# Head norms of a hybrid decoder trunk: one strip product of unsplit squares for two products of split squares, two strip results in one PSUM bank

## The chip, the cores and the metric

One core of one Trainium2 chip runs the whole kernel. The metric is the device time of one execution in microseconds (us); the number given for a kernel is the median of several executions. A profiled execution also gives the span from its first to its last instruction and the busy time of each engine: PE (TensorE, matmuls), PEld (its weight loads, which overlap with PE), DVE (VectorE), ACT (ScalarE), POOL (GpSimd) and SP (SyncE, which here only issues DMAs).

## What is computed

The trunk has one layer over 2048 tokens of width 1024. An input projection feeds four gated DeltaNet heads and four HGRN2 heads of width 128; each head's output is normed over its 128 channels and gated, the eight heads go through an output projection, and a squared-ReLU MLP and a gated embedding follow. The part that the change touches is the norm of a head's output:

```python
def gated_head_norm(o, w, z):
    o = o * lax.rsqrt(jnp.mean(o * o, axis=-1, keepdims=True) + EPS)
    return o * w.astype(jnp.float32) * jax.nn.silu(z)
...
o_a = gated_head_norm(o_a, gdn_norm[i], z_gdn)      # 4 DeltaNet heads
o_b = gated_head_norm(o_b, hgrn_norm[i], g_hg)      # 4 HGRN2 heads
mix = jnp.concatenate([o_a, o_b], axis=-1)
mix_out = jnp.einsum('btc,cd->btd', mix, w_out[i])
```

Everything is float32, and channels lie on partitions, so the mean over channels is a sum over the 128 partitions, which PE makes with a matrix of ones.

## The kernel before, in words

**Stages.** The 2048 tokens are four blocks q of 512. A first stage (to about 45 us) embeds and norms. The mixer stage (to about 1080 us) makes, for each block, 33 projections of 24 matmuls each (L1176; operands are split into a high and a low part, three matmuls for each of eight 128-row slices) and threads the heads' own work between them. Output projection (L1059, L1210 `mmo`), MLP (L1210 `u`, `d`) and gate (`mmg`) follow.

**Ticks.** PE's order is the order of the code. Each projection is cut into three ticks of eight matmuls (L1176). At the end of a tick the agenda runs one step of each generator that is due. A DeltaNet generator (`gdn_mixer`) and an HGRN2 generator (`hgrn_mixer`) start for each of the four head numbers of a block, 24 ticks after the ones before. `A_STEPS` lists the tick offsets of the DeltaNet steps, `B_STEPS` those of the HGRN2 steps; `A_LAST` and `B_LAST` are those of the last heads (q 3, head 3), where the projections have ended and output projections run instead. The first generators of the next block are a further three ticks off, because a block starts with the projection `ab`. SP's DMAs are issued in code order too. ACT, DVE and POOL are ordered by the scheduler of the language.

**A head's norm.** The last steps of both generators are `finish` and the steps that it takes from `norm_steps`. In the first, ACT squares the 512 columns of the head's output `pso` into `osq` (L613), DVE gates them into `og` (L614), for DeltaNet DVE adds a term (L616), and `split` makes the float32r pair `hl` of a rounded copy (ACT, L176) and a remainder (DVE, L177). In the second, two matmuls of 512 columns with a 128x128 matrix of ones sum both parts over the partitions (L283, L284), ACT copies one row of the result into row 0 of `osq` (L286), and SP stores it to `sd` in DRAM (L288). Then follow, a step each: load of `sd` as 128x4 (L291), scale and power -0.5 (L293 and L172), store to `rd` (L297), load of `rd` on all partitions (L257), multiplication (L622), store to `mixd` (L624). There are 32 such norms, 16 named `h` (HGRN2) and 16 named `g` (DeltaNet).

**Strips.** `strip` (L633) is a matmul with a stationary matrix of 32 columns that writes 32 of PSUM's 128 partitions, at a column position of the array given by `tile_position`. The mixers use strips for products of 32 or 64 columns; several run side by side in the four column positions. A float32 matmul shows as two instructions in the profile, a float32r one as one.

**Level 5 of the DeltaNet solve.** A step writes `psp` by strips, ACT copies it to `part` (L787). The next step writes `pst` and `psx` by strips, each in a quarter of a bank of its own; DVE copies `psx` into `xn` (L799), ACT copies `pst` into `xt` (L801). Level 6 reads `xn` (`psp6`), and one step later `xt` and ACT's `part` (L806) in `psd6`. Banks of the pool `pp` (three of them) go round in the order in which they are asked for.

Of the kernel before, what the change touches and what calls it, by code (L numbers as in the profile page):

```python
# [10 lines left out]
F32 = mybir.dt.float32  # L11
# [3 lines left out]
AF = mybir.ActivationFunctionType  # L15
# [5 lines left out]
P = 128  # L21
# [3 lines left out]
QT = 512  # L25
NQ = T // QT
NC = QT // P
# [4 lines left out]
SB = 32  # L32
# [22 lines left out]

A_STEPS = ((3, 6, 7, 8, 9, 10, 12, 14) + tuple(range(16, 24)) + (24, 26, 28, 30, 32, 34, 36)
           + tuple(o for c in range(38, 54, 4) for o in (c, c + 1.5, c + 2.5))
           + (53, 55, 57, 59, 60, 61, 65, 66))
I_STEPS = (22,)
B_STEPS = (24, 26, 28, 30, 32, 34, 36, 38, 40, 42, 44, 45, 46, 48, 50, 52, 53, 54, 58, 59)  # L60


A_AHEAD = (-12, -6)
# [2 lines left out]
A_FIRST = (3, 7, 8, 8, 9, 10, 12, 14) + tuple(range(16, 24)) + (24, 26, 29, 32, 34, 36, 37)  # L66

A_LAST = (A_STEPS[:16] + (24, 25, 27, 28, 29, 30, 31) + tuple(range(32, 44))
          + (44, 47, 49, 50, 51, 52, 54, 55))
B_LAST = tuple(range(24, 34)) + (35, 36, 37, 39, 41, 42, 43, 44, 46, 47)  # L70
LAST = 44


# [23 lines left out]
def trunk(ctx, tc, x, xT, pT, vecs, w_in, w_ab, gdn_a_log, gdn_dt_bias, w_out, w_up, w_down,  # L97
          w_ple, w_gate, consts, out):
    nc = tc.nc
    V, S, G, PE = nc.vector, nc.scalar, nc.gpsimd, nc.tensor  # L100
# [173 lines left out]
    yod = {q: [dr.tile([P, QT], F32, name=f"yod{q}_{d}") for d in range(KD)] for q in (0, 2, 3)}  # L274
    ple_r = [None] * NQ

    def norm_steps(acc, scale, eps, name, done, pool=None):

        hl = st.tile([P, 2, QT], F32R, tag="hl", name=f"hl_{name}", bufs=1)
        split(hl, V, acc)  # L280
        yield
        ps = bank(f"nrm_{name}", pool or pp)
        PE.matmul(ps, ones, hl[:, 0, :], start=True, stop=False)  # L283
        PE.matmul(ps, ones, hl[:, 1, :], start=False, stop=True)  # L284
        row = acc[0:1, :]
        S.activation(row, ps[0:1, :], AF.Copy)  # L286
        sd = dr.tile([1, QT], F32, name=f"sd_{name}")
        nc.sync.dma_start(sd, row)  # L288
        yield
        m = sm.tile([P, NC], F32, tag="m", name=f"m_{name}")  # L290
# [101 lines left out]
    with ExitStack() as ectx:  # L392
        es = ectx.enter_context(tc.tile_pool(name="es", bufs=1))
        with tc.manual_schedule(engines={mybir.EngineType.SP, mybir.EngineType.Activation, mybir.EngineType.DVE}):
# [44 lines left out]
            done = []  # L439
# [23 lines left out]
    with mixers as mctx:  # L463
# [145 lines left out]
        def finish(q, h, pso, zt, extra, eps, n):  # L609

            og = st.tile([P, QT], F32, tag="late", name=f"og_{n}")
            sq = st.tile([P, QT], F32, tag="acc", name=f"osq_{n}", bufs=3)
            S.activation(sq, pso, AF.Square, scale=P ** -0.5)  # L613
            V.tensor_tensor(og, pso, zt, ALU.mult)  # L614
            if extra is not None:
                V.tensor_tensor(sq, sq, extra, ALU.add)  # L616
            rd = []
            yield from norm_steps(sq, 1.0, eps, n, rd.append)
            yield
            rsb = spread_load(rd[0], n)  # L620
# [14 lines left out]
        def gdn_mixer(q, h, live):  # L635
# [139 lines left out]

            def half_bank(name):
                return bank(f"{name}_{n}", pp)[:, : QT // 4].rearrange("p (a i) -> p a i", a=2)

            psp = half_bank("psp5")
            for p in range(2):
                for g in range(NB):
                    strip(g, psp[rows_of(g), p, rows_of(1 - g % 2)], um[5][:, p, rows_of(g)],
# [1204 lines left out]
```

## Time and profile before

| what | value |
|---|---|
| median of 3 runs | 2638.28 us (2636.36 to 2641.67) |
| the profiled execution's own time | 2641.29 us |
| its span, first to last instruction | 2639.5 us |
| PE busy | 2602.8 us (99%) |
| DVE busy | 1965.0 us (74%) |
| ACT busy | 1463.3 us (55%) |
| granted TensorE clock, mean | 0.999 |

Busy time of PE is made from modelled ends of pipelined matmuls, so 99% means that PE is seldom without an instruction, not that it runs at its peak. What a piece of PE's work costs is read from the distance between the starts of neighbouring instructions; what it waits for from the idle time that the timeline shows in brackets with its releaser.

### The profile page before, as it was taken

The numbers are of one execution on the slowest core, as the hardware profiler recorded it, in microseconds if no ns is written. First come the engines' busy times: TensorE is split into PE (matmuls) and PEld (weight loads), VectorE is DVE, ScalarE is ACT, GpSimd is POOL, SyncE is SP. The second block draws the span as 40 slices with busy tenths as digits, with TensorE's granted clock in tenths as the row PEclk, the third lists the DMA queues.
The fourth block names the chain that finished last, engine by engine and source line by source line (L and its number), as shares of the span: only waits on it lengthen the run. The fifth ranks groups of instructions, "written<-read, shape, count | busy, mean of one in ns | idle before, by whom it ended". The sixth has DMA issues, their size and how long they took to land.

```text
span 2639.5 us, 43913 instructions
## 1 busy us (share of the span) xinstructions
PE 2602.8 (99%) x15593; PEld 2146.0 (81%) x15593; DVE 1965.0 (74%) x4032; ACT 1463.3 (55%) x2991; POOL 137.0 (5%) x147
## 2 busy tenths in 40 slices
PE   8999999999999999999999999999999999999999
PEld 6778788878878888787888888888888888888887
DVE  7778777776777777579988768767877765477775
ACT  7766655465555555566666465555454465565431
POOL 0000000000000000110000000001000001101000
PEclk9999999999999999999999999999999999999999
DMA  8877777767767675764675576665644375677663
GB/s 277 282 258 265 263 256 245 238 222 251 241 213 240 222 237 162 232 203 141 214 236 182 179 233 223 214 211 186 220 150 168 140 245 187 202 252 251 207 223 126
DMA packets 267788, 573.87 MB, mean 217 GB/s; under 512 B 55578, under 2 KB 60152, under 8 KB 250416
## 3 DMA queue, kind: packets, MB, share of 16 engines
q1 hardware_dynamic: 265264, 566.86, 64.5%
q0 software_dynamic: 2304, 4.20, 0.9%
q8 instruction: 123, 2.02, 0.3%
q14 instruction: 97, 0.79, 0.1%
HBM read 410.57 MB, written 160.37 MB: 216 GB/s over the span
## 4 chain that ended last, share of the span: by engine, by line
PE 61%; DMA 2%; issue 2%; DVE 2%; ACT 0%; POOL 0%; SPq 0%; DVEq 0%; POOLq 0%; ACTq 0%
PE d L1210 23%; PE u L1210 23%; PE mmg L1210 7%; PE mm L1176 4%; PE mmo L1059 1%; PE mme L203 1%; DMA yod<-yo 1%; DMA mixT<-mixd 0%; DMA rsb_g<-rd_g 0%; DMA yo<-in_xT_dram 0%; DVE t L177 0%; DMA rd_g<-m_g 0%; DVE acc_o L246 0%; POOL yo L1296 0%; DMA raw_out<-in_w_out_dram 0%
## 5 line engine op out<-in xcount | busy, mean ns | idle before, releaser
L1176 PE MATMUL mm<-xt,w 128*128 128x512 f32 x3072 | 785.5, 401 | 1.6 <-DVE acc_vg L571 0.7
L1176 PEld LDWEIGHTS mm<-xt,w 128*128 128x128 f32 x3072 | 552.8, 188 | 108.3 <-issue 2.1
L1210 PE MATMUL d<-db,da 128*128 128x512 f32 x2688 | 612.8, 389 | 0.0
L1210 PE MATMUL u<-t,wu 128*128 128x512 f32 x2604 | 591.2, 389 | 0.0
L1210 PEld LDWEIGHTS d<-db,da 128*128 128x128 f32 x2688 | 504.5, 188 | 104.8
L1210 PEld LDWEIGHTS u<-t,wu 128*128 128x128 f32 x2604 | 488.7, 188 | 101.5
L230 DVE TENSOR_TENSOR db<-db 128x512 fp32r<-128x512 f32 x224 | 159.5, 712 | 60.0 <-ACT db L229 59.0
L1612 DVE TENSOR_TENSOR u<-u,u 128x512 f32<-128x512 f32 x224 | 150.2, 681 | 52.0 <-PE u L1210 50.4
L229 ACT ACTIVATE db<-db 128x512 fp32r<-128x512 f32 x224 | 140.9, 629 | 67.4 <-DMA db<-hid 63.6
L1210 PE MATMUL mmg<-h2T,wg 128*128 128x512 f32 (+1 forms) x792 | 174.7, 383 | 0.0
L1210 PEld LDWEIGHTS mmg<-h2T,wg 128*128 128x128 f32 x792 | 145.5, 188 | 29.1
L1655 ACT ACTIVATE u<-u 128x512 f32<-128x512 f32 x128 | 80.7, 631 | 152.8 <-DVE u L1612 152.1
L177 DVE TENSOR_TENSOR da<-da 128x512 fp32r<-128x512 f32 x128 | 95.2, 743 | 91.3 <-ACT da L176 89.5
L176 ACT ACTIVATE da<-da 128x512 fp32r<-128x512 f32 x128 | 80.6, 630 | 127.8 <-DMA da<-sumd 100.9
L1210 PE MATMUL mmo<-mixT,w_out 128*128 128x512 f32 x600 | 140.0, 393 | 3.3 <-ACT w_out L176 2.0
L1210 PEld LDWEIGHTS mmo<-mixT,w_out 128*128 128x128 f32 x600 | 113.4, 190 | 28.8 <-DVE w_out L177 2.6
L176 ACT ACTIVATE wu<-a 128x512 fp32r<-128x512 f32 x124 | 75.0, 623 | 55.8 <-DMA a<-in_w_up_dram 52.9
L177 DVE TENSOR_TENSOR wu<-a,wu 128x512 fp32r<-128x512 f32 x124 | 85.9, 694 | 8.3 <-ACT wu L176 8.2
L177 DVE TENSOR_TENSOR da<-dr,da 128x512 fp32r<-128x512 f32 x96 | 68.2, 711 | 23.7 <-ACT da L176 22.2
L1656 ACT ACTIVATE u<-u 128x512 f32<-128x512 f32 x128 | 80.4, 628 | 3.0
L176 ACT ACTIVATE da<-dr 128x512 fp32r<-128x512 f32 x96 | 60.5, 630 | 31.9 <-DMA dr<-in_w_down_dram 21.7
L246 POOL TENSOR_TENSOR acc_y<-acc_y,sq_y 128x512 f32<-128x512 f32 x28 | 37.8, 1351 | 759.5 <-ACT sq_y L245 759.5
(401 smaller groups left out, 3675.4 us busy)
## 6 DMA issues: line engine op xcount, KB each, us to landing
w<-cache_in SPq DMA_DIRECT2D x96, 1024.0 KB
db<-hid SPq DMA_DIRECT2D x224, 256.0 KB
cache_in<-w SPq DMA_DIRECT2D x32, 1024.0 KB
hid<-u SPq DMA_DIRECT2D x128, 256.0 KB
da<-sumd SPq DMA_DIRECT2D x128, 256.0 KB
a<-in_w_up_dram SPq DMA_DIRECT2D x124, 256.0 KB
hid<-ht SPq DMA_DIRECT2D x96, 256.0 KB
dr<-in_w_down_dram SPq DMA_DIRECT2D x96, 256.0 KB
```

The lines of the kernel that those rows point to most:

```text
L176: S.activation(t[:, 0], raw, AF.Copy)
L177: eng.tensor_tensor(t[:, 1], raw, t[:, 0], ALU.subtract)
L203: PE.matmul(ps, a, b, start=i == 0, stop=i == n - 1)
L229: S.activation(t[:, 0], plain(t), AF.Copy)
L230: V.tensor_tensor(t[:, 1], plain(t), t[:, 0], ALU.subtract)
L246: eng.tensor_tensor(acc, acc, sq, ALU.add)
L1059: PE.matmul(ps, w[:, term // 2, k, :], xin[q][k][:, term % 2, :], start=i == 0, stop=i == 3 * KD - 1)
L1176: PE.matmul(ps, *terms[i], start=i == 0, stop=i == nt - 1)
L1210: PE.matmul(ps, a, b, start=start, stop=stop)
L1612: V.tensor_tensor(c[new], c[old], ps, ALU.add)
L1655: S.activation(c[k], c[k], AF.Relu)
L1656: S.activation(c[k], c[k], AF.Square)
```

## The change

The change has three parts.

1. The head norms (`strips=True`, called from `finish`) no longer split the squares. Four float32 strips, one for each 128 tokens, sum `osq` with 32 columns of the ones, each at its own column position; the sums of 128 tokens stand on 32 partitions each. ACT copies the 128x128 result, and in a step of its own SP stores four rows of it, one of each 32 partitions, to `sd`. The norm has one step more. All other norms (`norm_whole`) stay as they were.
2. The step lists get one entry more and other offsets, so that the strips come, where they can, just ahead of strips that were there already. From the first step to the store of `mixd` a DeltaNet norm takes 15 ticks instead of 13 and an HGRN2 norm 18 instead of 13.
3. `psx` and `pst` of level 5 are two parts of one bank.

```diff
-           + (53, 55, 57, 59, 60, 61, 65, 66))
+           + (53, 56, 57, 59, 61, 62, 63, 67, 68))
-B_STEPS = (24, 26, 28, 30, 32, 34, 36, 38, 40, 42, 44, 45, 46, 48, 50, 52, 53, 54, 58, 59)
+B_STEPS = (24, 26, 28, 30, 32, 34, 36, 38, 40, 42, 44, 45, 46, 52, 53, 55, 57, 58, 59, 63, 64)
...
-          + (44, 47, 49, 50, 51, 52, 54, 55))
-B_LAST = tuple(range(24, 34)) + (35, 36, 37, 39, 41, 42, 43, 44, 46, 47)
+          + (44, 46, 47, 49, 50, 51, 52, 54, 55))
+B_LAST = tuple(range(24, 34)) + (35, 36, 37, 38, 39, 41, 42, 43, 44, 46, 47)
...
-    def norm_steps(acc, scale, eps, name, done, pool=None):
+    def norm_in_strips(acc, name):
+
+        yield
+        ps = bank(f"nrm_{name}", pp)[:, :P]
+        for c in range(NC):
+            PE.matmul(ps[c * SB : (c + 1) * SB, :], ones.bitcast(F32)[:, :SB], acc[:, blk(c)], start=True, stop=True,
+                      tile_position=(0, c * SB))
+        S.activation(acc[:, :P], ps, AF.Copy)
+        sd = dr.tile([1, QT], F32, name=f"sd_{name}")
+        yield
+        nc.sync.dma_start(sd.rearrange("o (c n) -> (o c) n", n=P), acc[::SB, :P])
+        yield
+        return sd
+
+    def norm_whole(acc, name, pool):
...
+    def norm_steps(acc, scale, eps, name, done, pool=None, strips=False):
+
+        sd = yield from norm_in_strips(acc, name) if strips else norm_whole(acc, name, pool)
...
-            yield from norm_steps(sq, 1.0, eps, n, rd.append)
+            yield from norm_steps(sq, 1.0, eps, n, rd.append, strips=True)
...
-            def half_bank(name):
-                return bank(f"{name}_{n}", pp)[:, : QT // 4].rearrange("p (a i) -> p a i", a=2)
+            def half_banks(name, count):
+                t = bank(f"{name}_{n}", pp)[:, : count * QT // 4]
+                return t.rearrange("p (m a i) -> m p a i", m=count, a=2)
...
-            psx, pst = half_bank("psx5"), half_bank("pst5")
+            both = half_banks("psx5", 2)
+            psx, pst = both[0], both[1]
```

The step lists show how the order moves only in part; the built programs show it. On PE, before, the norm of the HGRN2 head 0 of block 1 stood between whole matmuls (`mm_1_2` is a projection of block 1, `psb_g`, `psc_g` and `of_g` belong to the DeltaNet state):

```order
L825 MATMUL psb_g_0_2_5047<-r_g_0_2_5006,xt_full 128x128
L1176 MATMUL mm_1_2_5042<-xt_1_3291,w_1_2_4883 128x512 x2
L1176 MATMUL mm_1_2_5042<-xt_2_3399,w_1_2_4883 128x512 x2
L283 MATMUL nrm_h_0_5055<-hl_h_0_5012,ones 128x512
L284 MATMUL nrm_h_0_5055<-hl_h_0_5012,ones 128x512
L1176 MATMUL mm_1_2_5042<-xt_2_3399,w_1_2_4883 128x512
L1176 MATMUL mm_1_2_5042<-xt_3_3402,w_1_2_4883 128x512 x3
L830 MATMUL psc_g_0_2_5081<-w_g_0_2_5049,kt_g_0_3835 128x128
```

In the changed program the same norm stands four ticks later on PE, at the head of strips of the next HGRN2 head (`of_h<-att_h` and `at_all<-hb_h`):

```order
L846 MATMUL psb_g_0_3_5115<-r_g_0_3_5079,xt_full 128x128
L1197 MATMUL mm_1_2_5101<-xt_4_3425,w_1_2_4955 128x512 x3
L1197 MATMUL mm_1_2_5101<-xt_5_3428,w_1_2_4955 128x512
L282 MATMUL nrm_h_0_5123<-osq_h_0_4996,ones 32x128 x4
L652 MATMUL of_h<-att_h_1_5041,one 32x4x16 x4
L652 MATMUL at_all<-hb_h_1_5042,qk_h_1_4784 32x2x16 x16
L1197 MATMUL mm_1_2_5101<-xt_5_3428,w_1_2_4955 128x512 x2
L851 MATMUL psc_g_0_3_5166<-w_g_0_3_5117,kt_g_0_3820 128x128
```

The four strips have joined a stretch of strips that was there before. The DeltaNet norm likewise moves from between whole matmuls to just ahead of the strips of `psx_g`. Of the 32 norms 23 join such a stretch. Nine do not: both norms of head 3 of blocks 0, 1 and 2, whose next heads start three ticks later, and three of the last block (`nrm_g` of head 2, `nrm_h` and `nrm_g` of head 3). On PE of the changed program, this is the HGRN2 norm of head 3 of block 1, alone among whole matmuls:

```order
L846 MATMUL psb_g_3_3_7386<-r_g_3_3_7350,xt_full 128x128
L1197 MATMUL mm_2_1_7360<-xt_4_6506,w_2_1_7217 128x512 x3
L1197 MATMUL mm_2_1_7360<-xt_5_6509,w_2_1_7217 128x512
L282 MATMUL nrm_h_3_7394<-osq_h_3_7273,ones 32x128 x4
L1197 MATMUL mm_2_1_7360<-xt_5_6509,w_2_1_7217 128x512 x2
L851 MATMUL psc_g_3_3_7405<-w_g_3_3_7388,kt_g_3_5995 128x128
```

Here the norm opens a stretch of strips of its own. On ACT the scheduler orders anew. Before, at the start of block 1, the DeltaNet head's exponentials (`cd_g`, `tail_g`, `e_g`, `gf_g`) and two loads of function tables stood ahead of `y_qg`, the convolved q that PE's strips `of_g<-y_qg` read:

```order
L669 ACTIVATE jk_g_0_3_3842,ssk_g_0_3827<-t_kg_0_3830 128x128
L649 ACT_TABLE_LOAD
L649 ACTIVATE cd_g_0_3776<-gf_g_0_3686 128x4
L652 ACTIVATE tail_g_0_3777<-tail_g_0_3777 128x8
L657 ACTIVATE e_g_0_3783<-e_g_0_3783,gcol_3707 128x128 x4
L658 ACTIVATE gf_g_0_3686<-gf_g_0_3686 128x512
L671 ACTIVATE kt_g_0_3835<-t_kg_0_3830,tail_g_0_3777 128x128 x4
L580 ACT_TABLE_LOAD
L580 ACTIVATE y_qg_0_3762<-acc_qg_0_3755 128x512
```

In the changed program `y_qg` comes ahead of the first of these table loads on ACT:

```order
L688 ACTIVATE jk_g_0_3_3827,ssk_g_0_3812<-t_kg_0_3815 128x128
L599 ACTIVATE y_qg_0_3745<-acc_qg_0_3738 128x512
L668 ACT_TABLE_LOAD
L668 ACTIVATE cd_g_0_3760<-gf_g_0_3667 128x4
L671 ACTIVATE tail_g_0_3761<-tail_g_0_3761 128x8
```

At the starts of blocks 2 and 3 `y_qg` stays behind them. In all 16 heads, since `psx` and `pst` share a tile, ACT's first copy into `xt_g` now waits for DVE's copies out of that bank into `xn_g`, which the code asks for first; before, it waited for PE alone.

More of the change, by code (lines that the diff above doesn't have):

```diff
@@ L289, in norm_steps @@
         yield
+        return sd
+    def norm_steps(acc, scale, eps, name, done, pool=None, strips=False):
+        sd = yield from norm_in_strips(acc, name) if strips else norm_whole(acc, name, pool)
         m = sm.tile([P, NC], F32, tag="m", name=f"m_{name}")
@@ L774, in pair_bank @@
                 return bank(f"{name}_{n}", pp)[:, : QT // 2].rearrange("p (a i) -> p a i", a=2)
-            def half_bank(name):
-                return bank(f"{name}_{n}", pp)[:, : QT // 4].rearrange("p (a i) -> p a i", a=2)
-            psp = half_bank("psp5")
+            def half_banks(name, count):
+                t = bank(f"{name}_{n}", pp)[:, : count * QT // 4]
+                return t.rearrange("p (m a i) -> m p a i", m=count, a=2)
+            psp = half_banks("psp5", 1)[0]
             for p in range(2):
```

## The prediction

> **What bounds the kernel now.** I read the table of busy time by stretch first. Its columns are the stretch, its length, then busy us of PE, PEld, DVE, ACT and POOL with their instructions, and last the granted clock, DMA share and GB/s.
>
> ```profile
> 60.00:1080.00 1020.00, 1005.47 (x8573) 829.53 (x8572) 763.89 (x2167) 593.73 (x1545) 58.20 (x66) 1.00 0.72 239
> 1080.00:1260.00 180.00, 174.58 (x754) 141.78 (x754) 142.55 (x220) 115.64 (x188) 15.63 (x17) 0.99 0.63 188
> 1260.00:2639.00 1379.00, 1375.12 (x6090) 1139.47 (x6088) 1011.87 (x1565) 712.40 (x1187) 57.95 (x44) 1.00 0.61 203
> ```
>
> In the mixer stage, the first row, PE is without work for only 1020 - 1005.5 = 14.5 us at full clock, while DVE (75%) and ACT (58%) have room. PE's order is fixed, so a microsecond of PE's work taken out of this stage comes off the end, as later stages are as full. Work taken from DVE and ACT counts only where PE waits for them. PE's waits in this stage come next: who waited, for whom, us in total, times, longest.
>
> ```profile
> PE of_g L633 <- ACT y_qg L580: 2.5, 3, 1.0
> PE psa_g L820 <- DVE S_g L832: 1.9, 4, 0.6
> PE at_all L915 <- DVE acc_vg L572: 1.8, 2, 1.3
> PE at_all L633 <- DVE att_h L933: 1.4, 4, 0.6
> PE psx_g L633 <- ACT osq_g L286: 1.4, 1, 1.4
> ```
>
> No single wait stands out; the norm's own name is in the last row.
>
> **The norm on PE, before.** The timeline of PE in a quiet head (start, duration, line, operation, count):
>
> ```profile
> 403.96 0.39 PE L283 MATMUL nrm_h<-hl_h,ones 128*128 128x512 f32 x1
> 404.19 0.39 PE L284 MATMUL nrm_h<-hl_h,ones 128*128 128x512 f32 x1
> 404.42 1.08 PE L1176 MATMUL mm<-xt,w 128*128 128x512 f32 x4
> 405.33 0.39 PE L830 MATMUL psc_g<-w_g,kt_g 128*128 128x128 f32 x2
> 405.55 0.39 PE L833 MATMUL of_g<-y_qg,S_g 128*128 128x128 f32 x2
> ```
>
> Durations overlap; the cost is from start to start. The norm's pair takes 404.42 - 403.96 = 0.46 us, a projection matmul (405.33 - 404.42)/4 = 0.23, and a float32 matmul of 128 columns (two instructions) 405.55 - 405.33 = 0.22.
>
> **Strips.** No strip of before moves 128 columns in all four column positions, but these groups come close. Each of the last three has eight strips, whose columns are 128, 96, 64 and 32 at the four positions and then 32, 64, 96 and 128, so 160 columns at each position:
>
> ```profile
> 427.55 0.43 PE L633 MATMUL psp_g<-xn_g,um 128*32 128x64 f32 x16
> 427.80 0.31 PE L633 MATMUL at_all<-qk_h,keys_h 128*32 128x32 f32 x16
> 427.93 0.47 PE L633 MATMUL of_g<-y_kg 128*32 128x128 f32 x16
> 428.21 0.47 PE L633 MATMUL of_g<-y_qg,y_kg 128*32 128x128 f32 x16
> 428.49 0.47 PE L633 MATMUL of_h<-y_kg 128*32 128x128 f32 x16
> ```
>
> Such a group takes 0.28 us. At the full matmul's rate, 0.22 us for 128 columns, 160 columns take 0.275: the four positions run fully side by side. The four strips of a norm, 128 columns at each position, are then 0.28 x 128/160 = **0.22 us**. The first row is eight strips of 64 columns, two at each position, again 128 columns: 427.80 - 427.55 = 0.25, so short strips lose a little. One after another the four would be 4 x 0.22 = 0.88, the other bound; I take 0.22, since the long strips of the groups are the nearer ones.
>
> The Trainium skill, page "TensorE: Matmul & The Clock Gate", section "Part 3: Packing small matmuls — row/col tiling", gives three column tiles a measured speedup of 2.38 and not 3. By it four strips would take about 0.22 x 3/2.38 = 0.28 us (an estimate from that page), and the change would save 32 x 0.06 = 1.9 us less. The groups above show no such loss.
>
> **Where strips begin and end.** Going from whole matmuls to strips and back has a price, seen in this stretch:
>
> ```profile
> 411.84 1.16 PE L1176 MATMUL mm<-xt,w 128*128 128x512 f32 x4
> 412.93 0.32 PE L633 MATMUL of_h<-att_h,one 128*32 128x64 f32 x8
> 413.06 0.48 PE L633 MATMUL at_all<-hb_h,qk_h 128*32 128x32 f32 x32
> 413.47 1.19 PE L1176 MATMUL mm<-xt,w 128*128 128x512 f32 x4
> ```
>
> From 411.84 to 413.47 are 1.63 us. Four projection matmuls take 0.91; the strips have 64 + 4 x 32 = 192 columns at each position, 0.34 us. What is left, 0.38 us, is the two changes. It is in the program already for the 23 norms that join a stretch; the nine alone pay it anew.
>
> **First term, PE's own work.** 23 norms: 0.46 - 0.22 = 0.24 us less each, 5.5 us. Nine norms: 0.22 + 0.38 - 0.46 = 0.14 us more each, 1.3 us. Sum **-4.2 us**. Moving the norm within the tick order adds nothing else to PE.
>
> **Second term, waits that go.** In the first head PE stood for 1.4 us, since the bank for `psx` still held the previous norm's result, which ACT copied late:
>
> ```profile
> 175.05 0.27 PE L633 MATMUL pst_g<-xt_g,part 128*32 128x32 f32 x8
> 176.69 0.22 PE L633 MATMUL psx_g<-part,xt_g 128*32 128x32 f32 x2 [1.37 <-ACT osq_g L286]
> 294.57 0.50 PE L283 MATMUL nrm_g<-hl_g,ones 128*128 128x512 f32 x1
> 295.37 0.49 PE L284 MATMUL nrm_g<-hl_g,ones 128*128 128x512 f32 x1 [0.29 <-DVE hl_g L177]
> 295.79 0.25 PE L548 MATMUL ps_gb<-cst,gb 36*128 36x36 f32 x1
> 309.82 0.49 PE L633 MATMUL of_g<-y_kg 128*32 128x128 f32 x16
> 311.31 0.49 PE L633 MATMUL of_g<-y_qg,y_kg 128*32 128x128 f32 x16 [1.00 <-ACT y_qg L580]
> ```
>
> With `psx` and `pst` in one bank and the norm right ahead, `psx` takes the bank of `psp`, which ACT has long read: -1.4. The next rows show the second matmul of a pair late, as DVE's half of the split came late: 295.79 - 294.57 = 1.22 us instead of 0.46. There is no split any more: -0.8. The last two rows are the start of block 1: 311.31 - 309.82 = 1.49 instead of 0.28. In the changed order of ACT `y_qg` comes ahead of a table load, four exponentials and more: -1.2. At the starts of blocks 2 and 3 it stays behind them, and I leave the other 1.5 us of this wait in. Sum **-3.4 us**.
>
> **Third term, work off ACT and DVE.** A norm loses these:
>
> ```profile
> L176 ACT ACTIVATE hl_g<-osq_g x16: 614/632/634, 170.3 to 1069.0; 128x512 fp32r<-128x512 f32 x16
> L177 DVE TENSOR_TENSOR hl_g<-osq_g,hl_g x16: 670/684/693, 171.2 to 1070.5; 128x512 fp32r<-128x512 f32 x16
> L286 ACT ACTIVATE osq_g<-nrm_g x16: 572/587/589, 176.1 to 1072.3; 1x512 f32<-1x512 f32 x16
> L827 ACT ACTIVATE w_g<-psb_g,cc_g 128x128 f32<-128x128 f32 x64 | 23.3, 364 | 79.8 <-PE psb_g L825 79.7
> ```
>
> The new copy is 128x128 from PSUM as in the last row, at most 0.36 us. ACT sheds 32 x (0.63 + 0.59 - 0.36) = 27 us, DVE 32 x 0.68 = 22 us, none of it on PE's path by itself. What it can shorten is the waits for DVE above, 1.9 + 1.8 + 1.4 = 5.1 us. Bounds 5.1 and 0; I take **0**, as the scheduler also orders DVE anew and these waits lie in heads crowded by other loads.
>
> **Fourth term, the new wait of ACT for DVE** (shared bank). The rows around level 5 of a quiet head:
>
> ```profile
> 424.02 0.90 ACT L801 ACTIVATE xt_g<-pst_g 32x64 f32<-32x64 f32 x4
> 425.98 0.45 DVE L799 COPY xn_g<-psx_g 32x64 f32<-32x64 f32 x2
> 428.05 0.57 ACT L806 ACTIVATE part<-psp_g 64x128 f32<-64x128 f32 x2 [0.94 <-PE psp_g L633]
> 433.03 0.43 PE L633 MATMUL psd_g<-xt_g,part 128*32 128x64 f32 x16
> ```
>
> ACT's copies would begin at 426.43, where DVE's end, instead of 424.02. Queued behind them on ACT are `xt_full`, later `keys` and `part`; PE waits for `part` at 433.03, 4.4 us after it is ready today. A shift of up to 2.4 us fits in. Where it doesn't fit, the nearest row is a wait of PE for `part`:
>
> ```profile
> 127.60 0.71 PE L633 MATMUL psd_g<-xt_g,part 128*32 128x64 f32 x16 [0.38 <-ACT part L806]
> ```
>
> Bounds: nothing, and 0.4 us in all 16 heads, 6.4 us. Nearest to nothing, by the 4.4 us; I take two heads, **+0.8 us**.
>
> **At no cost.** SP's store of `sd` no longer waits for ACT in the same step:
>
> ```profile
> SPq L288 <- ACT osq_h L286: 50.1, 15, 8.3
> ```
>
> SP issues weight reloads behind that wait, so they come earlier; PE hardly waits for weights, so I count nothing. The five DMAs of a norm stay five, at unchanged distances but for that one step; the longer lags hold `og` and `osq` longer, 18 of the 24 ticks between heads with two and three buffers, so no head waits for one. `mixd` of the last heads keeps its ticks, so the output projection loads it no later.
>
> **Sum.** -4.2 - 3.4 + 0 + 0.8 = -6.8 us. Against the profiled execution's 2641.29 us (span 2639.5 and 1.8 around it) that is 2634.5. That execution was 3.0 us above the median shown, within the runs' 2636.36 to 2641.67, so I forecast 2638.28 - 6.8 = **2631.5 us**. A measurement of this kernel can tell about 0.2%, 5.3 us, from no change: below 2633.0 is faster, above 2643.6 slower.
>
> **Rivals.**
> - *PE's term alone.* The scheduler's new orders of ACT and DVE bring as many waits as go: -4.2 us, 2634.1, within 0.2%. For it speaks that the waits are scattered over many causes; against it that three of them lose their cause. Chance 0.22.
> - *Lighter engines count.* The 5.1 us go as well: 2626.4. Against it: bursts, not averages, make these waits. Chance 0.10.
> - *Strips overlap less than the groups show:* each norm's strips take 0.25 us, as the eight of `psp_g` did, so the change saves 32 x 0.03 = 1.0 us less: 2632.5. Against it the 0.28 us groups, whose strips are as long as the norm's. Chance 0.05. The skill's page, above, speaks for this rival and would put it at 2633.4.
> - *ACT held by DVE: slower.* Place: `xt_g` behind `xn_g`, and on ACT behind it the copies that PE needs. It decides once DVE's copies come over 4 us later than ACT's do today, the slack at 433.03. With DVE 75% busy and other work ahead of those copies (a DMA-fed subtraction stands there at block starts), each head could lose 0.9 us: 16 x 0.9 = 14.4, less 7.6 gained, 6.8 us slower, 2645.1. Against it the 1.1 us by which DVE's copies (to 426.43) beat `psp_g` (427.55) in the rows above. Chance 0.08.
> - *The change doesn't do what it says:* the strips run one after another. 32 x (0.88 - 0.46) = 13.4, plus 9 x 0.38 = 3.4: 16.8 slower, 2655. The groups speak plainly against it. Chance 0.03.
>
> **How the numbers follow.** The forecast has 0.52. Its own spread, with terms three and four between their bounds, lies across the 2633.0 line, some seven parts in ten below. Faster: 0.37 of it, 0.10 of the lighter engines, 0.06 of the two rivals near the line, 0.53. Slower: 0.09 from the last two, cut a little for 2645.1 being near 2643.6. Same: 0.38. The range from 2626.0 (terms one to three) to 2638.5 (the first rival with most of the fourth term's upper bound) leaves out the last two rivals and part of the others, two in ten.
>
> **What would show it.** Right: starts 0.22 us apart from the norm's strips to the next strips; nine lone norms of about 0.6 us; no waits on `osq_g` or `hl_g` and two, not three, on `y_qg`. Wrong: strips 0.9 us long; PE waiting for `part`, `keys` or `xn_g` in many heads; or idle PE time in the stage above 14.5 us.

## The result, and the profile after

| | median | range | runs |
|---|---|---|---|
| before, beside it | 2638.57 us | 2634.13 to 2644.31 | 20 |
| changed | 2641.78 us | 2637.28 to 2648.33 | 20 |

The ratio is 1.0013 (95% interval 1.0007 to 1.0019): within the 0.2% that the prediction counts as no change, about 3 us slower (an interval of 1.8 to 5.0), and not 7 us faster as forecast. The changed kernel's profiled execution took 2639.28 us (span 2637.4), in the lower third of its runs, and alone would have shown a gain of 2 us on the profiled execution of before. A second profile comes from the repeat e12 below: 2645.81 us, the median of that run. I read both.

The stages of the changed kernel, columns as before:

```profile
60.00:1080.00 1020.00, 1006.91 (x8789) 829.20 (x8788) 749.84 (x2141) 568.14 (x1518) 59.25 (x67) 1.00 0.72 240
1080.00:1260.00 180.00, 172.81 (x743) 140.98 (x742) 140.71 (x217) 117.74 (x190) 14.27 (x16) 0.98 0.63 189
1260.00:2637.00 1377.00, 1373.02 (x6080) 1137.48 (x6078) 1009.48 (x1562) 708.19 (x1182) 58.30 (x44) 1.00 0.61 202
```

DVE lost 14 us in the mixer stage, where 22 were forecast, and ACT 26 of 27. PE still stands 13.1 us there, hardly less than the 14.5 of before, and in the second profile 16.5. The next stage is granted less clock, and the last row stands as it stood. PE's waits in the first of these stretches, first profile:

```profile
PE psa_g L841 <- DVE xs_g L767: 2.7, 1, 2.7
PE of_g L652 <- ACT y_qg L599: 1.5, 2, 1.1
...
PE psp_g L652 <- DMA xn_g<-xd_g: 1.2, 1, 1.2
...
PE mm L1197 <- DMA w<-cache_in: 1.0, 1, 1.0
```

The waits that were to go have gone: none on `osq_g` or `hl_g`, two on `y_qg`. Others stand in their place, and two of them end with a DMA, which none of before did.

**PE's own work** came out as forecast. A norm that joined a stretch of strips, and a lone one:

```profile
716.29 1.16 PE L1197 MATMUL mm<-xt,w 128*128 128x512 f32 x4
717.38 0.43 PE L282 MATMUL nrm_h<-osq_h,ones 128*32 128x128 f32 x8
717.62 0.29 PE L652 MATMUL of_h<-att_h,one 128*32 128x64 f32 x8
717.73 0.48 PE L652 MATMUL at_all<-hb_h,qk_h 128*32 128x32 f32 x32
718.14 1.19 PE L1197 MATMUL mm<-xt,w 128*128 128x512 f32 x4
...
593.44 1.16 PE L1197 MATMUL mm<-xt,w 128*128 128x512 f32 x4
594.53 0.43 PE L282 MATMUL nrm_h<-osq_h,ones 128*32 128x128 f32 x8
594.89 1.19 PE L1197 MATMUL mm<-xt,w 128*128 128x512 f32 x4
```

The stretch took 1.63 us without the norm and takes 718.14 - 716.29 = 1.85 with it: 0.22 us, as predicted. The lone norm takes 594.89 - 593.44 - 0.91 = 0.54 us against 0.60. So 23 x -0.24 + 9 x 0.08 = -4.8 us of PE's work.

**Where the profile says that the gain went.** The table follows the same projection matmul through the executions: its start in the trace, less its start in the profile of before (positive is later).

| start in before, us | 222 | 290 | 402 | 1004 | 1108 | 1255 | 2634 |
|---|---|---|---|---|---|---|---|
| changed, first profile | -2.6 | +2.2 | +1.3 | -4.5 | -4.6 | -2.3 | -2.1 |
| changed, second profile | -1.9 | +4.3 | +3.7 | +0.7 | +2.4 | +4.5 | +4.5 |

Both lose 5 to 6 us between 222 and 290 us, at the end of block 0, and 2 between 1108 and 1255. Over the blocks between, the first gained 5.8 us and the second only 3.0. The later loss lies at one place. At the first MLP matmul `u`, 1213.9 us in before, the differences are still -5.0 and +1.8; two hundred `u` matmuls on they are -2.3 and +4.5. These 2.7 us in both profiles are nearly as much as the 3 us of the result. The granted clock at the end of block 0 and in the output projection, first profile and then, for block 0 alone, second:

```profile
260.00:280.00 20.00, 18.51 (x96) 16.13 (x97) 19.64 (x52) 8.31 (x16) 0.00 (x0) 0.91 0.80 262
1120.00:1140.00 20.00, 16.65 (x66) 13.02 (x65) 13.88 (x23) 16.46 (x25) 2.08 (x3) 0.91 0.56 197
```

```profile
250.00:270.00 20.00, 17.18 (x80) 14.61 (x80) 15.75 (x51) 8.06 (x18) 0.00 (x0) 0.83 0.72 219
```

Of 20 us, 1.8 are lost to the clock at 0.91 and 3.4 at 0.83. Before has such a stretch in the output projection too, at 1117 us, so only what comes on top of it counts as new. How the first of these stalls came about in the first profile, on SP, DVE and PE:

```profile
240.85 1.23 SPq L531 DMA_DIRECT2D raw<-in_w_in_dram  x1
242.13 0.42 SPq L192 DMA_DIRECT2D cache_in<-w  x1
242.65 3.65 SPq L728 DMA_DIRECT2D ud_g<-u_g  x4
246.41 0.41 SPq L316 DMA_DIRECT2D rd_g<-m_g  x1
250.71 0.59 SPq L737 DMA_DIRECT2D sys_g<-ud_g  x1
```

```profile
257.36 0.28 DVE L749 TENSOR_TENSOR pr_g<-cst,sys_g 128x64 f32<-128x64 f32 x1 [4.48 <-DMA sys_g<-ud_g]
```

```profile
261.49 0.46 PE L841 MATMUL psa_g<-S_g,y_kg 128*128 128x128 f32 x2 [2.72 <-DVE xs_g L767]
```

The small stores `ud_g` leave right behind a load of 0.5 MB and a store of 1 MB. SP issues `sys_g` only once they have landed, DVE stands 4.5 us for it, the solve that follows is late, and PE stands 2.7 us. The same stores and the same load in before:

```profile
247.17 2.30 SPq L709 DMA_DIRECT2D ud_g<-u_g  x4
...
250.67 0.53 SPq L718 DMA_DIRECT2D sys_g<-ud_g  x1
```

There the stores left 4.5 us later, and SP could issue `sys_g` 1.2 us behind the last of them; here it took 4.4 us. So `sys_g` left at the same time in both, and the 2.6 us by which PE was ahead at 222 us had brought nothing forward. What held here is how fast SP's transfers landed, which is the first theory below in its first form. The prediction counted nothing for it, and no experiment changed this chain by itself. The experiments ask where else the gain went.

### The profile page after: what moved, and what is told of

It reads as the page before. It is cut to its first block, busy times and chain, and to the rows that moved or that the text cites. A ratio compares the mean times of both kernels' runs of the same rounds, so it can differ in the third digit from the quotient of the medians.

```text
span 2637.4 us, 44254 instructions
## 1 busy us (share of the span) xinstructions
PE 2600.8 (99%) x15785; PEld 2142.8 (81%) x15785; DVE 1946.3 (74%) x4000; ACT 1435.2 (54%) x2959; POOL 137.0 (5%) x147
## 4 chain that ended last, share of the span: by engine, by line
PE 71%; DMA 3%; DVE 3%; issue 2%; ACT 2%; SPq 0%; POOL 0%; DVEq 0%; ACTq 0%; POOLq 0%
PE d L1231 23%; PE u L1231 23%; PE mm L1197 12%; PE mmg L1231 7%; PE mmo L1080 1%; PE mme L203 1%; DMA yod<-yo 1%; DMA sys_g<-ud_g 0%; DMA rd_g<-m_g 0%; DMA b<-h1d 0%; DMA mixT<-mixd 0%; PE psa_g L841 0%; PE of_h L984 0%; PE pss_h L973 0%; PE of_h L983 0%
## 5 line engine op out<-in xcount | busy, mean ns | idle before, releaser
L176 ACT ACTIVATE da<-dr 128x512 fp32r<-128x512 f32 x96 | 60.5, 630 | 28.0 <-DMA dr<-in_w_down_dram 16.8
```

The source lines that it names most:

```text
L176: S.activation(t[:, 0], raw, AF.Copy)
```

## The experiments

The base of before differed from chip to chip (2638.6 to 2644.6 us), so each ratio is against before on the same chip. "Delta heads" in the expectations are the DeltaNet heads (`g`), "the other heads" the HGRN2 heads (`h`). The theories: the gain is lost to SP's queue (first as DMA's pace, later theory Q); to the shared bank; to the longer lags; to VectorE's late work (theory D); or strips save nothing.

The last two columns are sums of idle time in the profiled execution between 60 and 1080 us: PE's waits of every kind, and DVE's waits that ended with a DMA. The last column alone doesn't tell the time: e2, e12 and e16 have as much of it as e3 and stand within 4 us of before, while e4 has less and loses 16. The times follow PE's waits more closely.

| run | median less before, us | ratio (95%) | PE waits | DVE waits for DMA |
|---|---|---|---|---|
| before's own profile | | | 14.4 | 45.4 |
| e1 before, shared bank | +0.4 | 1.0003 (0.9992 to 1.0015) | 14.6 | 51.8 |
| e2 changed, two banks | +0.7 | 1.0007 (0.9997 to 1.0017) | 16.3 | 76.1 |
| e3 before, all lags long | +13.7 | 1.0051 (1.0037 to 1.0065) | 24.0 | 76.2 |
| e4 changed, lags short | +16.0 | 1.0057 (1.0041 to 1.0074) | 25.9 | 66.2 |
| e5 before, delta lags long | -5.7 | 0.9977 (0.9967 to 0.9988) | 10.1 | 50.5 |
| e6 changed, delta strips at 54 | +12.4 | 1.0051 (1.0036 to 1.0065) | 25.9 | 74.0 |
| e7 changed, HGRN2 tail tight | +20.2 | 1.0071 (1.0058 to 1.0084) | 27.8 | 99.9 |
| e8 delta strips at 54, HGRN2 as before | +5.7 | 1.0019 (1.0008 to 1.0030) | 21.1 | 58.5 |
| e9 before, HGRN2 lags long | +12.9 | 1.0050 (1.0034 to 1.0067) | 26.0 | 84.8 |
| e10 delta as changed, HGRN2 as before | -0.9 | 0.9997 (0.9989 to 1.0006) | 14.1 | 49.5 |
| e11 delta as changed, HGRN2 strips at 48 | +4.1 | 1.0015 (1.0006 to 1.0023) | 16.7 | 60.4 |
| e12 changed again | +3.3 | 1.0009 (1.0000 to 1.0018) | 15.7 | 80.9 |
| e13 as e9, HGRN2 DMAs by POOL | +78.2 | 1.0291 (1.0276 to 1.0306) | 62.4 | 135.8 |
| e14 changed, HGRN2 DMAs by POOL | +65.7 | 1.0245 (1.0231 to 1.0259) | 63.9 | 128.8 |
| e15 as e10, `sd_g` half a tick earlier | -2.4 | 0.9991 (0.9982 to 1.0000) | 14.6 | 50.1 |
| e16 changed, both `sd` half a tick earlier | +2.4 | 1.0006 (0.9997 to 1.0015) | 18.4 | 78.1 |
| e17 before less two DMAs | -1.8 | 0.9991 (0.9981 to 1.0002) | 13.0 | 47.2 |
| e18 as e9, less two DMAs | -3.0 | 0.9984 (0.9973 to 0.9995) | 18.5 | 43.5 |

### One part of the change at a time

**e1**, the shared bank put into before, and **e2**, taken out of the changed kernel:

```diff
-            psx, pst = half_bank("psx5"), half_bank("pst5")
+            both = half_banks("psx5", 2)
+            psx, pst = both[0], both[1]
```

> The kernel before with one part of the change alone: psx5 and pst5 in one PSUM bank; all norms stay whole. Theory 1 (the change saves about 7 us of PE work and waits over the blocks, and gives it back in block 0, where DMA sets the pace, and in new PE stalls near the end of the output projection, each with a stretch at half clock behind it): the bank plays no part, 0 within 1 us of before. Theory 2 (ACT's xt_g copies now wait for DVE's xn_g copies in the shared bank, and this is what ate the gain): 3 to 7 us slower than before. Theory 3 (the longer lags of the heads' tails ate it): 0 within 1 us.

> The changed kernel with psx5 and pst5 in two banks again; strips and lags stay. Theory 1: within 1 us of the changed kernel, so about 3 us slower than before. Theory 2 (the shared bank ate the gain): 3 to 7 us faster than the changed kernel, so 0 to 4 us faster than before. Theory 3 (the lags): as theory 1.

e1 gives +0.4 us, with an interval from -2 to +4, and e2 stands 2.5 us below the changed kernel's +3.2, each against before on its own chip. No cost of the bank is shown, and the 3 to 7 us that the second theory asked for show in neither run, though the top of e1's interval reaches 4.

**e3**, the longer lags alone, with whole norms:

```diff
-           + (53, 55, 57, 59, 60, 61, 65, 66))
+           + (53, 56, 59, 61, 62, 63, 67, 68))
-B_STEPS = (..., 45, 46, 48, 50, 52, 53, 54, 58, 59)
+B_STEPS = (..., 45, 46, 52, 55, 57, 58, 59, 63, 64)
```

> The kernel before, with whole norms at their pair of matmuls, but with the changed kernel's offsets for the heads' last steps (delta heads 53, 56, 59, 61, 62, 63, 67, 68, the other heads 46, 52, 55, 57, 58, 59, 63, 64). Theory 1: the later steps alone take away the waits of PE on nrm_g and psx (2.2 us of the trace of before) and cost nothing on PE: 0 to 2 us faster than before. Theory 3 (the lags move SP's stores, the loads behind them and the end of each block, and this ate the gain): 3 to 7 us slower than before.

It lost 13.7 us, twice what even the third theory asked for. The lags are not free, and since the changed kernel has the same lags and loses only 3 us, strips and bank together bring back about 10.

**e4**, strips with the lags of before, so that all 32 are lone:

```diff
-           + (53, 56, 57, 59, 61, 62, 63, 67, 68))
+           + (53, 55, 56, 57, 59, 60, 61, 65, 66))
-B_STEPS = (..., 45, 46, 52, 53, 55, 57, 58, 59, 63, 64)
+B_STEPS = (..., 45, 46, 48, 49, 50, 52, 53, 54, 58, 59)
```

> The changed kernel with strips and the shared bank, but with the offsets of before for the heads' last steps (strips at 55 and 48, no other strips in those ticks; stores at 66 and 59). All 32 norms are then lone strips. Theory 1, by its PE term: 32 lone norms at +0.14 us against the pair are +4.5 us where the changed kernel has -4.2, so about 6 to 9 us slower than the changed kernel, less what block 0 swallows of it (a quarter): +8 to +11 us on before. Theory 3 (the lags ate the gain): 0 to 4 us faster than the changed kernel. A rival to the PE term, that joined strips save nothing: the same as the changed kernel within 1 us.

Slower still, by more than PE's work: 32 lone norms at 0.08 are 2.6 us, while PE's waits grew by 11.5. The largest of them:

```profile
PE at_all L936 <- DVE acc_vg L591: 7.5, 2, 4.3
```

In this kernel one tick, not two, lies between the store of the sums and the load behind it; whether that is the reason is not shown. But short lags are no cure as such.

### Which heads, and which steps

**e5**, of e3 only the first line of the diff (the DeltaNet heads late), and **e9**, only the second (the HGRN2 heads late).

> The kernel before, whole norms, with the changed kernel's later offsets for the delta heads alone (53, 56, 59, 61, 62, 63, 67, 68); the other heads keep 46, 48, 50, 52, 53, 54, 58, 59. With both kinds late the same kernel lost 13.7 us. If the loss is shared by the kinds: 4 to 9 us slower than before. If the other heads' steps, which move by 4 to 5 ticks where the delta heads' move by 1 to 2, make it: within 2 us of before. If the delta heads make it: 11 to 14 us slower.

> The kernel before, whole norms, with the changed kernel's later offsets for the other heads alone (46, 52, 55, 57, 58, 59, 63, 64); the delta heads keep 53, 55, 57, 59, 60, 61, 65, 66. Both kinds late gave +13.7 us, the delta heads alone -5.7. If the two add up: 17 to 21 us slower than before. If the loss needs both (their steps fall into one tick): 0 to 8 us slower.

The DeltaNet heads' lags alone gain 5.7 us, which no theory had; the HGRN2 heads' lags alone lose 12.9, between the two ways expected. They don't add up: their sum is 7.2, and both together cost 13.7 (e3). DVE's waits for `rsb`, in before and then in e9:

```profile
DVE og_g L622 <- DMA rsb_g<-rd_g: 11.3, 8, 2.7
...
DVE og_h L622 <- DMA rsb_h<-rd_h: 4.0, 4, 2.0
```

```profile
DVE og_g L622 <- DMA rsb_g<-rd_g: 30.1, 13, 5.1
...
DVE og_h L622 <- DMA rsb_h<-rd_h: 19.9, 11, 3.6
```

The HGRN2 heads moved, but the DeltaNet heads wait most. The same head in both, first SP in before, then SP, DVE and PE in e9:

```profile
537.72 0.34 SPq L297 DMA_DIRECT2D rd_h<-m_h  x1
...
539.57 0.38 SPq L257 DMA_DIRECT2D rsb_h<-rd_h  x1
...
548.94 0.32 SPq L291 DMA_DIRECT2D m_g<-sd_g  x1
...
551.78 0.38 SPq L197 DMA_DIRECT2D w<-cache_in  x1
554.80 0.32 SPq L297 DMA_DIRECT2D rd_g<-m_g  x1
556.97 0.32 SPq L257 DMA_DIRECT2D rsb_g<-rd_g  x1
```

```profile
550.59 0.32 SPq L291 DMA_DIRECT2D m_h<-sd_h  x1
...
552.68 0.32 SPq L291 DMA_DIRECT2D m_g<-sd_g  x1
557.71 0.32 SPq L297 DMA_DIRECT2D rd_h<-m_h  x1
560.05 0.32 SPq L257 DMA_DIRECT2D rsb_h<-rd_h  x1
560.46 0.38 SPq L197 DMA_DIRECT2D w<-cache_in  x1
561.06 0.32 SPq L297 DMA_DIRECT2D rd_g<-m_g  x1
568.89 0.32 SPq L257 DMA_DIRECT2D rsb_g<-rd_g  x1
```

```profile
574.07 0.75 DVE L622 SCALAR_TENSOR_TENSOR og_g<-og_g,cols,rsb_g 128x512 f32<-128x512 f32 x1 [3.84 <-DMA rsb_g<-rd_g]
```

```profile
PE mm L1176 <- DVE acc_vg L571: 5.8, 3, 2.8
```

Before, SP had issued the last load of the `h` chain before that of `g` began. With the HGRN2 heads 4 to 5 ticks later the two chains interleave. `rd_g` now leaves 0.6 us behind a weight load of 1 MB, SP waits 7.8 us and not 2.2 until it may issue `rsb_g`, and DVE stands 3.8 us in front of work that PE needs (2.8 us there). This is one head; the largest sum of PE's waits in e9 is for `S_g`, 9.0 us against 1.9 in before. Over the 16 heads `rsb_g` left 16.8 us behind the norm's matmuls in before and 19.3 in e9, at the same offsets. SP's waits in front of `rsb_g`, in before and then in e9, say the same of the whole stage:

```profile
SPq L257 <- DMA rd_g<-m_g: 22.8, 11, 3.1
```

```profile
SPq L257 <- DMA rd_g<-m_g: 61.1, 14, 7.5
```

With those in front of `rsb_h` they are 48 us in before, 95 in e9 and 82 in e3. In the two profiles of the changed kernel they are 43 and 44: the hold that e9 shows is not in the changed kernel.

**e6**, the DeltaNet strips at 54, with the later steps of before; **e7**, the HGRN2 steps behind the strips drawn together; **e8**, DeltaNet as in e6 (the first diff) and the HGRN2 norms whole at their offsets of before, as in e10 below:

```diff
-           + (53, 56, 57, 59, 61, 62, 63, 67, 68))
+           + (53, 54, 55, 57, 59, 60, 61, 65, 66))
```

```diff
-B_STEPS = (..., 45, 46, 52, 53, 55, 57, 58, 59, 63, 64)
+B_STEPS = (..., 45, 46, 52, 53, 54, 55, 56, 57, 60, 61)
```

> The changed kernel with the delta heads' strips two ticks earlier, at 54, where other strips run too (psp and at_all, tick 16 of 24), so that their later steps return to the offsets of before (57, 59, 60, 61, 65, 66); the other heads as changed. The PE term is the changed kernel's. If the delta heads' lags cost: 3 to 8 us faster than the changed kernel, 0 to 5 us faster than before. If they cost nothing: within 1.5 us of the changed kernel. If the strips now wait for ACT's osq, one tick behind its end: 2 to 6 us slower than the changed kernel.

> The changed kernel with the other heads' steps behind the strips drawn together: 46, 52, 53, 54, 55, 56, 57, 60, 61 in place of 46, 52, 53, 55, 57, 58, 59, 63, 64; the strips stay joined at 52. If what the lags cost comes of how late these steps end: 2 to 6 us faster than the changed kernel. If it comes of their places alone: within 1.5 us. If SP now waits for a store's landing before the load behind it (one tick between them), with all its loads queued behind: 3 to 10 us slower than the changed kernel.

> Strips for the delta heads' norms alone, at 54 among other strips, with the offsets of before behind them; the other heads' norms whole, at their offsets of before; the shared bank stays. No step is later than in before. If strips among strips pay and lags cost: 12 to 16 joined norms at -0.24 us and part of the 2.2 us of waits that went, 2 to 5 us faster than before. If joined strips save nothing that reaches the end: within 1 us of before. If the strips wait for osq: 2 to 6 us slower than before.

All three lost, in the last of the ways expected of each, e6 and e7 by more than expected. e6 has SP's hold of e9 as well (102 us in front of `rsb_g` and `rsb_h`), e7 and e8 don't (40 and 50). In e8 PE stands for the squares, which one tick doesn't give DVE time to finish; in e7 DVE stands for `m_g`, and `at_all` behind it. One row each, e8 and then e7:

```profile
PE nrm_g L282 <- DVE osq_g L635: 7.3, 3, 3.7
```

```profile
PE at_all L936 <- DVE m_g L312: 7.2, 3, 3.8
```

### Parts joined

**e10** is the changed kernel with whole HGRN2 norms at the offsets of before; **e11** the same with HGRN2 strips at 48, lone; **e12** the changed kernel once more.

```diff
-B_STEPS = (..., 45, 46, 52, 53, 55, 57, 58, 59, 63, 64)
+B_STEPS = (..., 45, 46, 48, 50, 52, 53, 54, 58, 59)
...
-            yield from norm_steps(sq, 1.0, eps, n, rd.append, strips=True)
+            yield from norm_steps(sq, 1.0, eps, n, rd.append, strips=strips)
...
-            yield from finish(q, 4 + h, pso, zt, None, EPS, n)
+            yield from finish(q, 4 + h, pso, zt, None, EPS, n, False)
```

```diff
-B_STEPS = (..., 45, 46, 52, 53, 55, 57, 58, 59, 63, 64)
+B_STEPS = (..., 45, 46, 48, 49, 50, 52, 53, 54, 58, 59)
```

> The changed kernel with the delta heads as changed (strips among strips at 56, the late offsets) and the other heads' norms whole again at their offsets of before. If the other heads' lags are what ate the gain, and strips among strips pay: the -5.7 us of the delta heads' lags and 2 to 5 us of their strips, 7 to 12 us faster than before. If strips pay only where they make up for lags: 4 to 7 us faster than before. If delta strips cost as they did two ticks earlier: 0 to 6 us slower than before.

> The changed kernel with the delta heads as changed and the other heads' norms as strips with no other strips in their tick (48), so that their later steps keep the offsets of before (50, 52, 53, 54, 58, 59). By the PE term the 16 strips cost 0.14 us more than a pair each: 2 us slower than the same with whole norms, so 4 to 9 us faster than before. If lighter VectorE and ScalarE work (no split) counts as much: as fast as the whole ones or faster. If the lone strips cost what they did with all heads' offsets short (+16 us): 5 to 10 us slower than before.

> The changed kernel unchanged, for its ratio and its trace on the chip of these runs. The ratio of the first runs was 1.0013: 2 to 5 us slower than before. The stretches at half clock behind PE's stalls near 265 us and in the output projection are there again if they belong to the kernel, and not if they belong to one execution.

e12 repeats the ratio and the places of half clock. e10 lies between its ways, a gain of at least 4 us and a loss of 0 to 6: it stands level with before, so DeltaNet strips (with the shared bank) are about 5 us worse than whole norms at the same late offsets (e5, on another chip). e11, lone strips for the rest, is 5 us worse again, where PE's work asks for 16 x 0.08 = 1.3; by the profiles, 2.7 us of it fall at the first `u` matmuls, the place named above. One difference between e10 and e5 (19.0 us there) is in SP's waits, here of e10:

```profile
SPq L310 <- DMA sd_g<-osq_g: 65.0, 15, 8.2
```

### What about the lags costs

**e15** and **e16** store the sums half a tick earlier (`e10` and the changed kernel: 56.5 for 57; in e16 also 52.5 for 53).

> The kernel with the delta heads as changed and whole norms in the other heads at their offsets of before, with one step moved: the delta heads' store of the sums leaves half a tick behind the strips (56.5) and not a whole one (57). There SP stood 65 us at the load of m, waiting for that store to land, against 19 us with whole norms and late offsets, where the store leaves at 56. Theory Q: SP's wait falls to about 40 us and the time by 2 to 4 us, so 3 to 6 us faster than before. If SP's wait there holds nothing that is needed: the same within 1 us as with 57, so about 1 us faster than before.

> The changed kernel with both kinds' stores of the sums half a tick behind the strips (56.5 and 52.5) and not a whole tick (57 and 53). Theory Q: 1 to 4 us faster than the changed kernel. If that wait of SP holds nothing that is needed: within 1 us of it.

SP's wait in e15 stayed where it was, at 64.8 us, and the time moved by no more than its interval. So the half tick bought nothing, and this wait gives no sign of explaining the 5 us.

**e13** (as e9) and **e14** (as changed) move four DMAs of each HGRN2 norm to POOL:

```diff
+    def queue_of(name):
+        return G if name[0] == "h" and "_" in name else nc.sync
...
-        nc.sync.dma_start(rsb, rd.broadcast_to([P, QT]))
+        queue_of(name).dma_start(rsb, rd.broadcast_to([P, QT]))
```

> The kernel of the late other heads (whole norms, 46, 52, 55, 57, 58, 59, 63, 64; 13 us slower than before) with those heads' four DMAs between the norm and its use (the store of the sums, m, rd, rsb) issued by POOL and no longer by SP; the computation and the steps are the same. Theory Q (SP issues in order, and a step that waits there for a landing holds every load behind it; late steps put two heads' round trips into the same ticks, and VectorE then waits for rsb and sys): the loss falls to between 0 and 5 us, and VectorE's waits for rsb from 50 us to under 25. Theory D (VectorE's own late work, rsqrt and og's scaling, holds the delta heads' chain): still 10 to 15 us slower than before. A third way: POOL, held at those waits, is late for its own m_g and rk_g, 5 to 15 us slower.

> The changed kernel with the other heads' four DMAs between the norm and its use issued by POOL. Theory Q: VectorE's waits for DMA between 60 and 1080 us fall from 69 to 81 us to about 50, and the time by 3 to 8 us, so 0 to 5 us faster than before. Theory D: within 1.5 us of the changed kernel. POOL late for its own work: 3 to 10 us slower than the changed kernel.

The third way, and far worse. The row of DVE in e13:

```profile
DVE og_h L625 <- DMA rsb_h<-rd_h: 79.2, 14, 9.4
```

As a test of theory Q these two tell nothing, since `rsb_h` now came late by another road. They fit the last link, from a late `rsb` to PE, without singling it out: in e13 DVE's waits for DMA rose by 90 us over before, PE's waits by 48, and the time by 78.

**e17** and **e18** take two of the DMAs away and keep the steps (e18 with the second line of e3's diff). They leave out the reciprocal root in the HGRN2 heads, whose `og_h` is scaled with itself:

```diff
+        if done is None:
+            return
         rd = dr.tile([1, QT], F32, name=f"rd_{name}")
...
-            rsb = spread_load(rd[0], n)
+            rsb = spread_load(rd[0], n) if h < 4 else og
```

> The kernel before with two DMAs of the other heads' norms left out (the store rd and the load rsb of 16 heads), so that og_h is scaled with itself in place of the reciprocal root: that part of the output isn't computed. VectorE's and ScalarE's instructions stay in number, size and place. It is the base for the next kernel. Theory Q (SP's queue in order): SP waits less for landings, 0 to 6 us faster than before. Theory D (VectorE's own late work): within 2 us of before.

> The same leaving out (rd and rsb of the other heads; og_h scaled with itself), with the late offsets of the other heads (46, 52, 55, 57, 58, 59, 63, 64). With the two DMAs these late offsets cost 13 us. Theory Q: SP no longer stands at rd_h and rsb_h in the ticks where the delta heads need it, VectorE's waits for rsb_g fall from 30 us to under 12, and the late offsets cost 0 to 4 us on the base. Theory D: VectorE's rsqrt and scaling stand where they stood, and the late offsets cost 10 to 14 us on the base. In between, 5 to 9 us: both.

Without `rd_h` and `rsb_h` the late offsets cost nothing: 0.9984 against 0.9991, where they cost 0.50% with them. SP's wait in front of `rsb_g`, 61.1 us in e9, is 22.5 in e18. DVE's wait for `rsb_g` in e18, and the place of one scaling:

```profile
DVE og_g L624 <- DMA rsb_g<-rd_g: 16.5, 10, 3.2
```

```profile
713.66 0.75 DVE L624 SCALAR_TENSOR_TENSOR og_h<-og_h,cols 128x512 f32<-128x512 f32 x1
```

30.1 us have become 16.5, not the under 12 that theory Q asked for, but no more than the 15.9 of e17; and `rsb_g` leaves 16.4 us behind the norm's matmuls, as early as in before. The second row limits the test: with nothing to wait for, the scheduler put this scaling right behind the gating, some 17 ticks ahead of its offset, so it didn't stay in place, as the expectation had it. So half of theory D is untested. Of the late root only a small scaling is DVE's (L293); the power itself is POOL's (SP's waits name POOL for `m_g`, L172), so theory D had it on the wrong engine. What is shown is that the price hangs on the two DMAs together with the scaling that waits for them; how it divides between SP's held loads, DVE standing for `rsb_h` itself (19.9 us in e9) and the scaling's late place is not told apart. e18's profiled execution was the slowest of its twelve, so its waits may lie above the usual.

## Why the prediction was wrong

- **PE's own work, -4.2 us: right.** 0.22 us for a joined norm, 0.54 for a lone one, -4.8 us in all.
- **Waits that go, -3.4 us: right by name, not in sum.** The three causes left. PE's waits in the stage went from 14.4 us to 13.0 in one profile and 15.7 in the other, as new ones came. That is the condition of the first rival, but its 4.2 us of gain did not come either.
- **Lighter ACT and DVE, 0, bounds to -5.1: not settled.** From e3 to the changed kernel, at the same lags, strips and bank bring about 10 us. PE's work is half of that. The rest may be the lighter engines or the store's new place, with which SP's hold in front of `rsb` goes from 82 us (e3) back to 43.
- **Shared bank, +0.8 us: not contradicted.** e1 has +0.4 us (-2 to +4), and the slower rival, with 14.4 us for ACT held by DVE, is out.
- **"At no cost": the step that failed.** It reads that the five DMAs of a norm "stay five, at unchanged distances", and that "no head waits for one". That looked along one norm and at its buffers (of which one did hold a head up, for 2.4 us in e3). It did not set the norm's DMAs beside those of the other head in the same ticks, on the one queue that issues both in order. In place of 0 the late offsets alone cost +13.7 us (e3), by the HGRN2 heads (e9, +12.9), while the DeltaNet heads' lags gain 5.7 (e5). The changed kernel stands at +3.2, so strips, their extra step and the bank bring about 10 of the 13.7 back, and the 6.8 us are gone. No rival of mine held this mechanism.
- **Where the changed kernel itself lost its gain.** SP's hold of e3 and e9 is not in its profiles (43 and 44 us, before 48). They lose 5 to 6 us at the end of block 0, in the first profile because SP's small stores landed late (above), in the second behind a wait of DVE for `rsb_h` (2.5 us), and 2.7 us at the first `u` matmuls, both places at which the sum had nothing. So the step is shown by e3 and e9; how the loss came about in the changed kernel is read from two profiles and not tested.
- **The signs.** In the first profile every sign named as right was there: 0.22 us, lone norms of 0.54, no waits on `osq_g` or `hl_g`, two on `y_qg`. Of the wrong ones, PE's idle time above 14.5 us came in the second profile alone (16.5). The signs watched PE's own instructions, and the loss came from elsewhere. The range's lower end, terms one to three, comes to 2625.6 us and not 2626.0, which changes nothing.
- **The rule on packed strips**, the Trainium skill, page "TensorE: Matmul & The Clock Gate", section "Part 3: Packing small matmuls — row/col tiling": three column tiles gain 2.38 and not 3. The 0.22 us above speak against such a loss for these 128-column strips, as the prediction had it.

Open are the 5 us between e5 and e10, and two stalls from 1080 us on, which both profiles of the changed kernel have and for which I tried nothing (`nrm_o` for ACT's `hl_o`, `u` for `w_u`). The second is the place of the 2.7 us. First the changed kernel, then before:

```profile
PE nrm_o L1262 <- ACT hl_o L176: 3.1, 1, 3.1
PE u L1231 <- ACT w_u L176: 2.1, 1, 2.1
```

```profile
PE u L1210 <- ACT w_u L176: 0.9, 1, 0.9
```

The wait for `w_u` is 1.6 to 2.6 us long in eight of the nine profiles of kernels with HGRN2 strips (e6 has 1.0), with a stretch at half clock behind it in all of these but e2, and at most 0.9 us in the profiles without them, before among them. Why ACT is later there, measured by PE, is not known.

The best kernel found is e5: whole norms, two banks, and only the DeltaNet heads' steps one to two ticks later, 0.9977 of before.

## What to carry to other kernels

Where one engine issues all DMAs in order and waits for landings between them, a step that is moved takes its DMAs into other company: write down, tick by tick, which round trips and which large transfers share that queue, before a lag is called free. Try a change of places apart from the change that asked for it; here the places alone held +13.7 and -5.7 us, more than the new instruction form. And with runs that scatter by 10 us, one profile says what happens, not how much it is worth.

## What the hardware showed unexpectedly

**A small store behind a large transfer.** From the starts on SP I took, for each `rd_g`, the time until SP issued `rsb_g`, by whether a transfer of 0.5 or 1 MB had been issued less than 1 us ahead of it: in before 5.4 us (5 heads) against 3.1 (11), in e9 6.9 (11) against 5.5 (5). This time holds SP's own other work too, and in e9 it is longer in both groups. The Trainium skill, page "DMA: Bandwidth & Descriptors", section "Queues, rings and completion order", says that SP's DMAs share one ring on each DMA engine, whose descriptors are taken in order. The trace agrees, as far as an interval of issue times can.

**The clock after a short stall.** The trace records the granted clock in stretches; each stretch at half speed between the first and the last 50 us of an execution is 3.41 us long, or twice that, so 1.7 us of work are lost in each 3.41. They stand behind stalls of PE of 2.7 us (261.49 above), 3.1 (`nrm_o`) and 2.1 (`u`), and in before behind one of 2.0 us at 1116. But not every such stall has one: the 2.8 us in e9 (at 574 us), 3.0 in e3 (at 277) and 3.2 in e11 (at 273) are followed by full clock. The Trainium skill, page "TensorE: Matmul & The Clock Gate", section "What's actually happening", asks for an idle window of about 3.4 us; here shorter stalls were enough at some places and not at others. So a stall of 2 to 3 us costs its own length, and at some places 1.7 us more; what decides is not shown.
